# Two-layer mixture-of-experts trunk on one core: rows stored by index into expert slots while routing, plain loads and stores per expert, results fetched by token at the end

## The chip, the cores and the metric

The kernel runs on one core of a Trainium2 chip. The time is that of the device for one execution, in microseconds (us). Engines: PE multiplies matrices, DVE and ACT work on vectors, POOL (GpSimd) on vectors and on DMAs by index, SP only issues DMAs. The DMAs of all queues are carried out by the core's 16 DMA engines.

## The reference, cut to what matters

Two layers work on 512 latent tokens and 256 context tokens of width 1024. Each layer has a token mixer and then a mixture of 32 experts, of which each token takes two. In the last layer the experts see the latent tokens alone.

```python
def hier_moe(h, rg_w, rg_b, re_w, re_b, w_gate, w_up, w_down):
    g_top = jnp.argmax(g_logits, axis=-1)
    ...
    top_vals, top_idx = lax.top_k(e_in, TOP_K)
    top_w = jax.nn.softmax(top_vals, axis=-1) * g_w
    expert_idx = g_top[:, None].astype(jnp.int32) * EXPERTS_PER_GROUP + top_idx.astype(jnp.int32)
    ...
    def run_block(args):
        tok, e = args
        xb = h_pad[tok]
        return (jax.nn.silu(xb @ w_gate[e]) * (xb @ w_up[e])) @ w_down[e]
    ...
    return jax.ops.segment_sum(y_buf, buf_tok, num_segments=T + 1)[:T].astype(h.dtype)
...
        x = x + g2 * y[:B * T].reshape(B, T, D)
        ctx_h = ctx_h + cg2 * y[B * T:].reshape(B, n_ctx, D)
...
    return rms_norm(x, final_norm_g)
```

## The kernel before

The order of the work on each engine is written out by hand. All weights come through one list of 1 MB loads on SP's queue: `pump` issues the next of them into the pool R, seven buffers of 8 KB per partition, as far ahead as `st["depth"]` allows. Each expert has six such loads, 6.29 MB. A load becomes two half-precision parts: ACT writes the high part (L1335), DVE the low part (L1340), and each product of the gate and up matrices is three matmuls (`mm3`, L418 to L420). Half of the down matrix is used as it came (L1283).

A layer runs so. `out_and_route` makes the mixer's output projection tile by tile (128 tokens, six tiles in layer 0, four in layer 1), the residual, the second norm and the router. For each tile `choose` finds the two experts on DVE; `positions` counts with small matmuls which place a token has in its expert. The normalized rows, a high and a low half-precision part of 2 KB each, are stored in token order to the DRAM tensor `hs[l]` on SP's queue (L865), the residual stream to `xs[l]` on ACT's.

`moe` then runs 32 experts. An expert has 96 slots (`CAP`); experts with more tokens go through `overflow_blocks`, which this input doesn't need. Expert 0's rows are picked by matmuls. For the others, two tables turn the routing round: `slots` builds on DVE and PE the list of tokens for each slot, `values` the weight of each slot. POOL fetches an expert's rows by index (`fetch`, L1214; slots without a token move nothing), PE turns them (L1226), and gate, up and down follow, each expert's down product beside the next one's gate. `down_out` scales by the slot's weight on ACT, POOL builds the gate row for latent and context tokens (L1294, L1295, layer 0 alone), multiplies by it (L1303) and adds the rows to `xs[l]` by an indexed DMA that reads and writes (L1307). At the end the latent rows are loaded from `xs[l]`, and the last expert's rows are added by matmuls with a selection matrix (`add_last`, L1456, L1459). After layer 0 the rows are normalized and transposed for the next mixer (L488, L476, L464); after layer 1 they are normalized and written out (L1704).

The pools: G, 14 large buffers for converted weights, fetched rows (`xg`) and results (`ye`); R, seven raw loads; W, small tiles.

## Time and profile before

| | before |
|---|---|
| median of 3 runs | 1858.94 us (1855.53 to 1868.47) |
| the profiled execution | 1856.79 us |
| its span, first to last instruction | 1855.0 us |
| busy: PE, DVE, ACT, POOL | 1609.5, 1330.5, 1020.3, 1032.4 us |
| moved by DMA | 542.31 MB, mean 292 GB/s |

Busy times are of one engine each and lie beside each other; only the work that the end waits for sets the time. The gate activation of expert 0 (L1261) starts at 376.0 us in layer 0 and at 1248.4 in layer 1, that of expert 31 at 952.9 and 1814.8. The stretches in the rows below are cut at gate activations.

### The profile page before, as it was taken

How to read it: one execution, taken by the hardware profiler on the slowest of the kernel's cores; microseconds unless marked ns; L12 is line 12 of the kernel's file. 1: busy time of each engine (PE TensorE's matmuls, PEld its weight loads, DVE VectorE, ACT ScalarE, POOL GpSimd, SP SyncE). 2: the span in 40 equal slices, each digit the busy share in tenths (PEclk: the TensorE clock that was granted, in tenths of full speed). 3: DMA queues.
4: the chain of work that ended last, by engine and by line, in shares of the span. 5: the costliest groups of instructions: out<-in, count | busy, mean ns of one | idle time of the engine just before them, and what ended most of it. 6: DMA issues, size and time to landing. Idle time of an engine off the chain costs nothing. (4 is left out here: it accounts for less than half of the span.)

```text
span 1855.0 us, 43386 instructions
## 1 busy us (share of the span) xinstructions
PE 1609.5 (87%) x19059; PEld 1179.5 (64%) x19059; DVE 1330.5 (72%) x1451; ACT 1020.3 (55%) x1040; POOL 1032.4 (56%) x526
## 2 busy tenths in 40 slices
PE   6999999868888888888878999887888888889885
PEld 3567775556666666666654677566676666667663
DVE  5665567878789767777776877787767776666764
ACT  4433342446665666666654444346666666666662
POOL 1222234547898889998894333252554555454553
PEclk9999999889999999999998999988999999989998
DMA  9644564579998999999983455667999999999993
GB/s 386 234 159 155 183 227 153 174 231 375 382 359 326 383 364 344 370 358 361 364 318 143 136 196 180 269 213 268 377 366 348 378 354 369 352 357 357 360 348 116
DMA packets 123293, 542.31 MB, mean 292 GB/s; under 512 B 17594, under 2 KB 18666, under 8 KB 87000
## 3 DMA queue, kind: packets, MB, share of 16 engines
q1 hardware_dynamic: 105384, 507.87, 73.0%
q0 software_dynamic: 14000, 20.54, 4.7%
q10 hardware_dynamic: 3712, 11.04, 1.5%
q8 instruction: 153, 2.51, 0.5%
q14 instruction: 44, 0.36, 0.1%
...
## 5 line engine op out<-in xcount | busy, mean ns | idle before, releaser
L1340 DVE SCALAR_TENSOR_TENSOR wlo<-raw,whi 128x2048 f16<-128x2048 f32 x248 | 589.3, 2410 | 216.5 <-ACT whi L1335 216.4
L1335 ACT ACTIVATE whi<-raw 128x2048 f16<-128x2048 f32 x248 | 472.8, 1910 | 316.8 <-DMA raw<-in_exp_w_up_dram 279.3
L420 PEld LDWEIGHTS <-wlo 128*128 128x128 f16 x4512 | 458.3, 102 | 175.6 <-issue 144.5
L418 PEld LDWEIGHTS <-whi 128*128 128x128 f16 x4512 | 459.1, 102 | 45.9 <-issue 16.6
L419 PEld LDWEIGHTS <-whi 128*128 128x128 f16 x4512 | 458.8, 102 | 40.4 <-issue 11.2
L419 PE MATMUL pgate<-xl,whi 128*128 128x96 f16 x2048 | 308.1, 220 | 132.8 <-ACT xl L1234 132.5
L418 PE MATMUL pgate<-xh,whi 128*128 128x96 f16 x2048 | 312.1, 220 | 5.0 <-DVE xh L1233 4.8
L1303 POOL TENSOR_TENSOR ye<-ye,modrow 96x512 f32<-96x512 f32 x62 | 163.0, 2628 | 264.4 <-ACT ye L1287 264.4
L420 PE MATMUL pgate<-xh,wlo 128*128 128x96 f16 x2048 | 308.1, 220 | 0.0
L418 PE MATMUL pup<-xh,whi 128*128 128x96 f16 x2048 | 266.3, 206 | 0.0
L420 PE MATMUL pup<-xh,wlo 128*128 128x96 f16 x2048 | 266.1, 206 | 0.0
L419 PE MATMUL pup<-xl,whi 128*128 128x96 f16 x2048 | 266.0, 206 | 0.0
L1283 PE MATMUL pdn<-raw,sg 128*96 128x512 f32 x512 | 243.9, 599 | 0.0
L1307 POOL DMA_INDIRECT xs<-ye,si x63 | 171.4, 2721 | 21.5 <-POOL ye L1303 17.3
L1340 DVE SCALAR_TENSOR_TENSOR wd<-raw,wd 128x2048 f16<-128x2048 f32 x64 | 163.2, 2549 | 16.5 <-ACT wd L1335 16.3
L1294 POOL TENSOR_SCALAR ye<-modrow,sv 96x1024 f32<-96x1024 f32 x32 | 162.3, 5073 | 1.4
L1303 POOL TENSOR_TENSOR ye<-ye 96x512 f32<-96x512 f32 x62 | 134.7, 2183 | 49.3 <-ACT ye L1287 47.3
L1283 PEld LDWEIGHTS pdn<-raw,sg 128*96 128x96 f32 x512 | 85.2, 166 | 89.7 <-issue 71.1
L1335 ACT ACTIVATE wd<-raw 128x2048 f16<-128x2048 f32 x64 | 122.2, 1910 | 21.1 <-DMA raw<-in_exp_w_down_dram 21.1
L418 PE MATMUL pdn<-wd,at 128*96 128x512 f16 x256 | 100.1, 391 | 20.8 <-ACT at L1271 11.1
L1214 POOL DMA_INDIRECT xg<-hs,si x62 | 94.3, 1521 | 36.8 <-issue 23.2
L405 DVE SCALAR_TENSOR_TENSOR wlo<-raw,whi 128x2048 f16<-128x2048 f32 (+1 forms) x36 | 82.8, 2305 | 40.2 <-ACT whi L404 40.2
...
## 6 DMA issues: line engine op xcount, KB each, us to landing
raw<-in_exp_w_gate_dram SPq DMA_DIRECT2D x128, 1024.0 KB
raw<-in_exp_w_up_dram SPq DMA_DIRECT2D x128, 1024.0 KB
raw<-in_exp_w_down_dram SPq DMA_DIRECT2D x128, 1024.0 KB
...
```

Of the source, the lines that this page charges most:

```text
L405: V.scalar_tensor_tensor(lo, t, WS, hi, op0=ALU.mult, op1=ALU.subtract)
L418: T.matmul(o, lhsT=lh, rhs=rh, start=first, stop=False)
L419: T.matmul(o, lhsT=lh, rhs=rl, start=False, stop=False)
L420: T.matmul(o, lhsT=ll, rhs=rh, start=False, stop=last)
L1214: Q.indirect_dma_start(out=xg[0:CAP], out_offset=None, in_=hs[l], in_offset=bass.IndirectOffsetOnAxis(ap=si, axis=0), bounds_check=(6 - 2 ...
L1283: T.matmul(pt[0:CAP, :], lhsT=sg[:, f, :], rhs=raw[:, f - 2, sl], start=False, stop=(f == 3))
L1294: Q.tensor_scalar(gn, g2r[0:CAP, 1, :], ctx, None, op0=ALU.mult)
L1303: eng.tensor_tensor(yn, yn, gs[n], op=ALU.mult)
L1307: Q.indirect_dma_start(out=xs[l], out_offset=bass.IndirectOffsetOnAxis(ap=si, axis=0), in_=yg[0:CAP, 0, :], in_offset=None, bounds_check=6 ...
L1335: A.activation(hi[:, sl, :], t, AF.Copy, scale=WS)
L1340: V.scalar_tensor_tensor(lo, t, WS, hi, op0=ALU.mult, op1=ALU.subtract)
```

## The change

The DRAM tensor `hs` now has a row of 4 KB for each of 32 x 96 slots and serves both layers. `clear_rows` fills it with zeros in the first mixer, in eight DMAs on ACT's queue. `positions` runs tile by tile and gives each token its two slots (`si`; beyond the end for a token without a place), and `dispatch` stores the tile's rows there with two indexed DMAs from POOL; the store in token order remains, to `hn[l]`. `slots`, `values` and the tables are gone; the token's two weights are made at e = 4 (`weights`). `fetch` is a plain load of the expert's 96 rows, on SP's queue (the first two on POOL's). `down_out` scales by a constant, and `keep_rows` stores all 96 result rows plainly to `ys[l]` on ACT's queue. At the end `collect` fetches for each tile the two result rows of every token by index, and `combine` weights them, adds them, multiplies by the gate row and adds the residual: one pass on ACT and three on DVE per tile. The last expert's rows still come through matmuls in the latent tiles (`sel_last`); in layer 0 two context tiles are combined behind them. `finish` puts each tile's final norm between the combinations. The depth of the weight loads falls to 2 near the end of a layer, since the collected rows lie in pool R.

```diff
-    hs = [pd.tile([(6 - 2 * l) * 128, 2 * D], F16, name=f"hs{l}") for l in range(DEPTH)]
+    hs = pd.tile([NE * CAP, 2 * D], F16, name="hs")
+    hn = [pd.tile([(6 - 2 * l) * 128, 2 * D], F16, name=f"hn{l}") for l in range(DEPTH)]
+    ys = [pd.tile([NE * CAP, D], F32, name=f"ys{l}") for l in range(DEPTH)]
...
+    def clear_rows(q):
+
+        e0, r = 8 * (q // 2), q % 2
+        nc.scalar.dma_start(
+            out=hs.rearrange("(e p) (r d) -> p e r d", p=CAP, r=2)[:, e0:e0 + 8, r, :],
+            in_=zrow.unsqueeze(1).to_broadcast([CAP, 8, D]))
...
+            if l == 0 and 5 <= n < 13:
+                clear_rows(n - 5)
...
+        def dispatch(i):
+
+            for k in range(2):
+                Q.indirect_dma_start(
+                    out=hs, out_offset=bass.IndirectOffsetOnAxis(ap=rt.si[:, i, k:k + 1], axis=0),
+                    in_=h2[i // 2][:, i % 2].rearrange("p r d -> p (r d)"), in_offset=None,
+                    bounds_check=NE * CAP - 1, oob_is_err=False)
+            store_rows(i)
...
             if i > 1:
-                store_rows(i - 2)
+                rt.positions(i - 2)
+                dispatch(i - 2)
             resid(i, 1, V)
...
-        store_rows(i - 1)
         rt_mm(i, True)
-        rt.positions(0, i)
+        rt.positions(i - 1)
...
         low = norm2(i, True)
-        rt.positions(i, nt)
+        dispatch(i - 1)
+        rt.positions(i)
         make_sel(pe, rt.posm[:, :, 0:1], (i,), V)
         low()
-        store_rows(i)
+        dispatch(i)
...
+        def positions(self, i):
+
+            t, oh = self.tmp[:, i], self.oh
+            pos = P([128, 512], "pos")[:, 0:32]
+            for j in range(i + 1):
+                T.matmul(pos, lhsT=(tri16 if j == i else ones16), rhs=oh[:, j, :], start=(j == 0), stop=(j == i))
+            o = t[:, 120:184].rearrange("p (k e) -> p k e", k=2)
+            pk, sf, dead = self.pk[:, i], self.sf[:, i], t[:, 184:186]
+            V.tensor_tensor(o, o, pos.unsqueeze(1).to_broadcast([128, 2, 32]), op=ALU.mult)
+            V.tensor_reduce(pk, o, axis=AX.X, op=ALU.add)
+            V.tensor_scalar(dead, pk, CAP - 0.5, 65536.0, op0=ALU.is_gt, op1=ALU.mult)
+            V.scalar_tensor_tensor(sf, self.ef[:, i], float(CAP), pk, op0=ALU.mult, op1=ALU.add)
+            V.tensor_tensor(sf, sf, dead, op=ALU.add)
+            V.tensor_copy(self.si[:, i], sf)
+            V.scalar_tensor_tensor(self.posm[:, i], pos, 1.0, oh[:, i], op0=ALU.add, op1=ALU.mult)
...
+    def fetch(xg, e, eng=nc.sync):
+
+        eng.dma_start(out=xg[0:CAP], in_=hs[e * CAP:e * CAP + CAP, :])
...
-    def scatter_rows(l, yg, si):
-        Q.indirect_dma_start(
-            out=xs[l], out_offset=bass.IndirectOffsetOnAxis(ap=si, axis=0),
-            in_=yg[0:CAP, 0, :], in_offset=None, bounds_check=6 * 128 - 1, oob_is_err=False,
-            compute_op=ALU.add)
+    def down_out(pt, y, n):
+        A.activation(y[0:CAP, n * 512:(n + 1) * 512], pt[0:CAP, :], AF.Copy, scale=IWS)
+
+    def keep_rows(l, e, y):
+        nc.scalar.dma_start(out=ys[l][e * CAP:e * CAP + CAP, :], in_=y[0:CAP])
+
+    def collect(l, yt, rows, i, n):
+
+        for k in range(2):
+            Q.indirect_dma_start(
+                out=yt[:, k], out_offset=None, in_=ys[l][0:n * CAP],
+                in_offset=bass.IndirectOffsetOnAxis(ap=rows[:, i, k:k + 1], axis=0),
+                bounds_check=n * CAP - 1, oob_is_err=False)
+
+    def combine(xx, yt, w, i, g2row):
+
+        A.activation(yt[:, 0], yt[:, 0], AF.Copy, scale=w[:, i, 0:1])
+        V.scalar_tensor_tensor(yt[:, 0], yt[:, 1], w[:, i, 1:2], yt[:, 0], op0=ALU.mult, op1=ALU.add)
+        V.tensor_tensor(yt[:, 0], yt[:, 0], g2row, op=ALU.mult)
+        V.tensor_tensor(xx, xx, yt[:, 0], op=ALU.add)
...
-        rt.slots()
         for e in (1, 2):
-            fetch(l, xg[:, e % 2], slot(e))
+            fetch(xg[:, e % 2], e, Q)
...
-        rt.values()
         hi_(1, 1, 1)
...
+            yg = rows_of(e)
+            if e + 3 < NE:
+                fetch(xg[:, (e + 1) % 2], e + 3)
             if e == NE - 2:
-                st["depth"] = NR - 2
+                st["depth"] = 2
...
-            scatter(l, yg, slot(e), gs, Q)
+            down_out(pt, yg, 1)
+            keep_rows(l, e, yg)
...
         overflow_blocks()
+        yts = []
+        for i in range(4):
+            yts.append(R([128, 2, D], F32, "yt"))
+            collect(l, yts[i], rt.sa, i, NE - 1)
...
+        for i in range(4):
+            xx = xl[i // 2][:, i % 2]
+            combine(xx, yts[i], rt.wa, i, g2r[:, 0])
+            for n in range(2):
+                sl = slice(n * 512, (n + 1) * 512)
+                pt = P([128, 512], "pcm")
+                T.matmul(pt, lhsT=selT[0:CAP, i * 128:(i + 1) * 128], rhs=yh[n][0:CAP], start=True, stop=True)
+                V.tensor_tensor(xx[:, sl], pt, xx[:, sl], op=ALU.add)
+            finish(i, xx)
+        finish(4, None)
+        if nv == 2:
+            for i in (4, 5):
+                yt = R([128, 2, D], F32, "yt")
+                collect(l, yt, rt.sa, i, NE)
+                combine(xl[2][:, i % 2], yt, rt.wa, i, g2r[:, 1])
```

Where the change moves instructions, the order shows it at three places. POOL's row from the end of layer 0's routing into the expert loop, before (`h` are the normalized rows, `xg` the fetched ones, `ye` the results, `modrow` the gate rows):

```order
L861 TENSOR_TENSOR h_2_3367<-h2f,h_2_3367 128x512
L1486 MEMSET xg 96x2048
L1214 DMA xg<-hs_81,si_2720 96x2048 x2
L1498 TENSOR_TENSOR modrow<-modrow 128x1024
L1294 TENSOR_SCALAR ye<-modrow,sv_2721 96x1024
L1295 TENSOR_TENSOR ye<-ye,modrow 96x1024
L1303 TENSOR_TENSOR ye<-ye 96x512 x2
L1307 DMA xs_79<-ye,si_2720 768x1024
```

And with the change (`rsi` are the slots of the tokens; L403 and L1331 are the norm's power step and the load of the overflow count at the loop's end):

```order
L883 DMA hs<-h_1_3186,rsi_2735 3072x2048 x2
L403 TENSOR_TENSOR ss<-ss,mhalf 128x1
L863 TENSOR_TENSOR h2f<-h2f,modrow 128x512
L864 TENSOR_TENSOR h2f<-h2f,modrow 128x512
L873 TENSOR_TENSOR h_2_3435<-h2f,h_2_3435 128x512
L883 DMA hs<-h_2_3435,rsi_2735 3072x2048 x4
L1204 DMA xg<-hs 96x2048 x2
L1331 TENSOR_LOAD nov_2738
```

The two fetches now stand behind four indexed stores, the last of which needs the last tile's slots, and nothing of POOL is left in the loop.

POOL's row from the end of layer 0's loop (a branch) to the transposes of the next layer, before:

```order
L1355 UNCONDITIONAL_BRANCH
L1446 TENSOR_TENSOR yh<-ye,yh 96x512
L1307 DMA xs_79<-ye,si_2720 768x1024
L400 TENSOR_TENSOR ss<-ss,mhalf 128x1 x4
L448 TENSOR_TENSOR hTl<-hmod,hTh 128x512 x4
```

And with the change (`yt` are collected rows):

```order
L1337 UNCONDITIONAL_BRANCH
L1282 DMA yt<-ys_84,rsa_2736 128x1024 x8
L403 TENSOR_TENSOR ss<-ss,mhalf 128x1 x4
L1282 DMA yt<-ys_84,rsa_2736 128x1024 x4
L451 TENSOR_TENSOR hTl<-hmod,hTh 128x512 x4
```

Eight gathers for the latent tiles come first, and the four of the context tiles stand behind the four power steps of the latent tiles' norms.

DVE's row from the last down product of layer 1 to the end, before:

```order
L1444 SCALAR_TENSOR_TENSOR ye<-pdn,sv_15018,modrow 96x512 x2
L1446 TENSOR_TENSOR yh<-ye,yh 96x512
L1459 TENSOR_TENSOR xl<-pcm,xl 128x512 x8
L399 TENSOR_SCALAR ss<-ss 128x1 x2
L1704 SCALAR_TENSOR_TENSOR xl<-xl,ss,fg 128x1024
L399 TENSOR_SCALAR ss<-ss 128x1
L1704 SCALAR_TENSOR_TENSOR xl<-xl,ss,fg 128x1024
L399 TENSOR_SCALAR ss<-ss 128x1
L1704 SCALAR_TENSOR_TENSOR xl<-xl,ss,fg 128x1024 x2
```

And with the change, for the first two of four tiles:

```order
L1565 SCALAR_TENSOR_TENSOR yh<-pdn,modrow 96x512 x2
L1290 SCALAR_TENSOR_TENSOR yt<-yt,rwa_14842 128x1024
L1291 TENSOR_TENSOR yt<-yt,modrow 128x1024
L1292 TENSOR_TENSOR xl<-xl,yt 128x1024
L1578 TENSOR_TENSOR xl<-pcm,xl 128x512 x2
L402 TENSOR_SCALAR ss<-ss 128x1
L1290 SCALAR_TENSOR_TENSOR yt<-yt,rwa_14842 128x1024
L1291 TENSOR_TENSOR yt<-yt,modrow 128x1024
L1292 TENSOR_TENSOR xl<-xl,yt 128x1024
L1578 TENSOR_TENSOR xl<-pcm,xl 128x512 x2
L402 TENSOR_SCALAR ss<-ss 128x1
L1700 SCALAR_TENSOR_TENSOR xl<-xl,ss,fg 128x1024
```

All of `combine` stands behind the last down product's passes (`yh`), and each tile has three passes of 1024 columns more.

## Rows read from the trace of the kernel before

**Rows 1.** The page: busy time, 40 slices of PE and DMA.
```profile
PE 1609.5 (87%) x19059; PEld 1179.5 (64%) x19059; DVE 1330.5 (72%) x1451; ACT 1020.3 (55%) x1040; POOL 1032.4 (56%) x526
...
PE   6999999868888888888878999887888888889885
...
DMA  9644564579998999999983455667999999999993
```

**Rows 2.** 26 experts per layer: us, PE, PEld, DVE, ACT, POOL, clock, DMA, GB/s.
```profile
457.10:939.70 482.60, 412.11 (x5939) 321.79 (x5938) 375.55 (x254) 310.81 (x261) 438.85 (x159) 0.95 0.98 362
1321.20:1798.30 477.10, 412.13 (x5937) 323.26 (x5936) 331.31 (x252) 310.31 (x261) 249.69 (x107) 0.95 0.97 360
```

**Rows 3.** Waits in the stretch of layer 1: total us, times, longest.
```profile
ACT whi L1335 <- DMA raw<-in_exp_w_up_dram: 130.0, 37, 5.8
```

**Rows 4.** DMA queues, layer 0: packets, MB, share of 16 engines.
```profile
q1 hardware_dynamic: 29186, 164.02, 88.8%
q0 software_dynamic: 5824, 9.72, 8.3%
```

**Rows 5.** DMA queues in the stretch of layer 1.
```profile
q1 hardware_dynamic: 29211, 164.06, 90.7%
q0 software_dynamic: 5842, 6.72, 5.9%
```

**Rows 6.** PE where the loops start, timeline: start, us, [idle before].
```profile
393.40 0.71 PE L1116 MATMUL ptab<-rwt,ph 128*96 128x96 f16 x6 [12.57 <-DVE rwt L1145]
...
395.90 1.48 PE L1226 MATMUL pgx<-ident,xg 96*128 96x96 f16 x16
...
1261.21 1.48 PE L1226 MATMUL pgx<-ident,xg 96*128 96x96 f16 x16
```

**Rows 7.** GB/s in 40 slices of 376 to 424 us, 1.2 us each.
```profile
GB/s 393 432 440 434 420 335 321 311 253 270 317 294 96 0 0 0 0 0 7 0 14 198 396 280 116 300 423 75 143 277 314 277 202 249 263 406 335 406 365 427
```

**Rows 8.** DVE before the first expert of layer 0, timeline.
```profile
369.61 0.69 DVE L860 TENSOR_TENSOR h<-h2f,h 128x512 f16<-128x512 f32 x1
...
373.07 0.35 DVE L1097 TENSOR_REDUCE rtmp<-rtmp 128x6 f32<-128x192 f32 x1
```

**Rows 9.** POOL's groups in layer 0's stretch: busy us, mean ns, idle before.
```profile
L1307 POOL DMA_INDIRECT xs<-ye,si x25 | 75.7, 3026 | 7.0 <-POOL ye L1303 7.0
...
L1214 POOL DMA_INDIRECT xg<-hs,si x26 | 39.6, 1524 | 8.0 <-issue 7.0 <-PE pgate L420 0.9
```

**Rows 10.** SP and POOL at the start of layer 1, timeline.
```profile
1240.65 1.48 SPq L865 DMA_DIRECT2D hs<-h  x2
...
1250.43 2.16 POOL L1214 DMA_INDIRECT xg<-hs,si  x1 [9.06 <-DMA hs<-h]
```

**Rows 11.** Stretches of the mixer and of two routing tiles, layer 0.
```profile
150.00:250.00 100.00, 100.00 (x905) 72.57 (x903) 58.24 (x87) 37.13 (x59) 24.08 (x24) 1.00 0.40 146
313.00:328.70 15.70, 15.70 (x87) 8.62 (x86) 12.35 (x23) 3.48 (x6) 9.12 (x7) 1.00 0.17 67
328.70:344.20 15.50, 12.22 (x71) 7.20 (x69) 12.29 (x20) 5.17 (x7) 8.06 (x6) 1.00 0.38 128
```

**Rows 12.** DVE at the end of layer 0, timeline.
```profile
977.45 1.41 DVE L1444 SCALAR_TENSOR_TENSOR ye<-pdn,sv,ye 96x512 f32<-96x512 f32 x2 [5.17 <-POOL ye L1295]
...
988.38 0.75 DVE L488 TENSOR_SCALAR xl<-xl,ss 128x1024 f32<-128x1024 f32 x1 [0.63 <-POOL ss L400]
...
992.58 1.53 DVE L464 TENSOR_SCALAR hmod<-xT,abT 128x512 f32<-128x512 f32 x2 [0.60 <-PE xT L476]
```

**Rows 13.** DVE at the end of layer 1, timeline.
```profile
1836.62 0.75 DVE L1444 SCALAR_TENSOR_TENSOR ye<-pdn,sv,modrow 96x512 f32<-96x512 f32 x1 [2.27 <-PE pdn L1283]
...
1838.67 4.87 DVE L1459 TENSOR_TENSOR xl<-pcm,xl 128x512 f32<-128x512 f32 x8
...
1844.29 1.28 DVE L1704 SCALAR_TENSOR_TENSOR xl<-xl,ss,fg 128x1024 f32<-128x1024 f32 x1 [0.63 <-POOL ss L400]
...
1847.28 2.48 DVE L1704 SCALAR_TENSOR_TENSOR xl<-xl,ss,fg 128x1024 f32<-128x1024 f32 x2 [0.38 <-POOL ss L400]
```

More of the change, by code (lines that the diff above doesn't have):

```diff
@@ L1075, in choose @@
             V.scalar_tensor_tensor(self.oh[:, i], iot32, ef[:, 1:2], o1, op0=ALU.is_equal, op1=ALU.add)
-        def positions(self, i0, i1):
-            nt, oh = i1 - i0, self.oh
-            pos = P([128, 512], "pos")[:, 0:nt * 32].rearrange("p (t e) -> p t e", e=32)
-            for i in range(i0, i1):
-                for j in range(i + 1):
-                    T.matmul(pos[:, i - i0, :], lhsT=(tri16 if j == i else ones16), rhs=oh[:, j, :],
-                             start=(j == 0), stop=(j == i))
-            V.scalar_tensor_tensor(self.posm[:, i0:i1], pos, 1.0, oh[:, i0:i1], op0=ALU.add, op1=ALU.mult)
@@ L1111, in table @@
-        def table(self, rs, n):
-            nt = self.nt
-            pt = P([128, 512], "ptab")[0:CAP, 0:n]
-            for k in range(2):
-                for i in range(nt):
-                    T.matmul(pt, lhsT=self.ph[k][:, i, :], rhs=rs[k][:, i],
-                             start=(k == i == 0), stop=(k == 1 and i == nt - 1))
-            return pt
-        def values(self):
-            nt, tmp, oh, v4 = self.nt, self.tmp, self.oh, self.v4
-            g0, o1, o2, tv = tmp[:, :, 56:60], tmp[:, :, 120:152], tmp[:, :, 152:184], tmp[:, :, 184:216]
+            V.tensor_scalar(o2, iot32, ef[:, 1:2], None, op0=ALU.is_equal)
@@ new lines, in overflow_blocks @@
+                    m, t2 = (wt[:, 2 * nt * k:2 * nt * k + 2 * nt].rearrange("p (t k) -> p t k", k=2) for k in range(2))
+                    pb, vf = wt[:, 4 * nt:5 * nt], wt[:, 5 * nt:6 * nt]
+                    V.tensor_scalar(m, rt.ef, bc[:, 1:2], None, op0=ALU.is_equal)
+                    V.scalar_tensor_tensor(t2, rt.pk, 1.0, m, op0=ALU.add, op1=ALU.mult)
+                    V.tensor_tensor(pb, t2[:, :, 0], t2[:, :, 1], op=ALU.add)
+                    V.tensor_scalar(pb, pb, bc[:, 3:4], None, op0=ALU.subtract)
@@ L1382, in overflow_blocks @@
+                    for q in range(3):
+                        V.tensor_copy(vb[:, :, q + 1], vf)
+                        V.tensor_tensor(vf, vf, vb[:, :, q + 1], op=ALU.subtract)
                     pe = W([128, nt, CAP], F16, "pe")
-                    make_sel(pe, pb, range(nt))
-                    sv, si = slot_vals(pe, lambda i: vb[:, i, :], nt)
-                    fetch(l, xg[:, 0], si[0:CAP, :1])
+                    make_sel(pe, pb.unsqueeze(2), range(nt))
+                    sv, si = slot_vals(pe, vb, nt)
@@ L1449, in add_last @@
-        def add_last(selT, yh):
-            for i in range(4):
-                for n in range(2):
-                    sl = slice(n * 512, (n + 1) * 512)
-                    pt = P([128, 512], "pcm")
-                    for r in range(2):
-                        T.matmul(pt, lhsT=selT[0:CAP, i * 128:(i + 1) * 128], rhs=yh[0:CAP, r, sl],
-                                 start=(r == 0), stop=(r == 1))
-                    xx = xl[i // 2][:, i % 2, sl]
-                    V.tensor_tensor(xx, pt, xx, op=ALU.add)
@@ L1514, in moe @@
                 xe = turned(xt_)
-            down_out(pt, weight(0), yg[:, 0, :], n)
+            down_out(pt, yg, n)
+        keep_rows(l, 0, yg)
         lo_()
-        scatter(l, yg, slot(0), gs, Q)
         pgt = P([128, 4, CAP], "pgate")
@@ L1534, in moe @@
         hi_(2, 1, 1)
-        for e in (3, 4):
-            fetch(l, xg[:, e % 2], slot(e))
+        fetch(xg[:, 1], 3)
         xe = xn
-        pes = None
         for e in range(1, NE):
@@ L1566, in moe @@
             pt = down_mm(w, raw, at, sgd, 0)
-            down_out(pt, weight(e), yg[:, 0, :], 0)
+            down_out(pt, yg, 0)
             if nx2:
@@ L1587, in moe @@
             xe = xn
+            if e == 4:
+                rt.weights()
             if e == 8:
@@ L1673, with finish0 @@
     h2, rt, pe0 = out_and_route(0, mix, job, 6)
-    xt = moe(0, h2, rt, pe0, 6)
-    xt.append(G([128, 2, D], F32, "x"))
-    nc.sync.dma_start(out=xt[2], in_=xs[0][512:768, :].rearrange("(t p) d -> p t d", p=128))
-    norm_in_place(xt[:2])
+    xt = [G([128, 2, D], F32, "x") for _ in range(2)]
+    fin = []
+    def finish0(i, xx):
+        if i < 0:
+            return
+        if i < 4:
+            ss = rms(xx)
+            nc.scalar.dma_start(out=xs[0][i * 128:(i + 1) * 128, :], in_=xx)
+        if i:
+            V.tensor_scalar(xt[(i - 1) // 2][:, (i - 1) % 2], fin[0], fin[1], None, op0=ALU.mult)
+        if i < 4:
+            fin[:] = xx, ss
+    xt.append(moe(0, h2, rt, pe0, 6, finish0))
     hT = alloc_hT()
```

259 lines of the change are left out of this document (101 added, 158 removed).

## The prediction

> **What bounds the kernel now.** I read the page first: no engine is full over the span, PE is highest at 87%, but the slices show the DMA engines at nine tenths in two long runs with PE below nine [rows 1]. These are the expert loops. Stretches cut from one expert's gate activation to another's, 26 experts each, show the DMA engines busy for 98% and 97% of the time, PE for 412 of 482.6 and 412 of 477.1 us [rows 2]. So an expert takes 18.56 us in layer 0 and 18.35 in layer 1, while PE works 15.9 of it. The waits say the same from the engines' side: ACT's conversion of the weights waits for their DMA, 130 us in layer 1 alone [rows 3]. POOL, the engine that the change empties, is busy for 439 of 482.6 us in layer 0 but only 250 in layer 1 [rows 2], and the loop is as slow there: POOL doesn't set the pace, and its 17 us per expert buy nothing when they go. **The loops are bound by the DMA engines, so the change is priced in DMA time.**
>
> The queue views split that time. In layer 0, q1 (weights) has 88.8% of the engines for 164.02 MB, q0 (indexed fetch and adding scatter) 8.3% for 9.72 MB; in layer 1, q1 90.7%, q0 5.9% for 6.72 MB [rows 4, 5]. Per expert: q1 16.5 and 16.6 us for 6.31 MB, which is 383 and 379 GB/s; q0 1.54 us for 0.37 MB and 1.08 us for 0.26 MB. q0 is dear per byte (243 GB/s), but moves only rows that hold a token.
>
> **The change part by part**, against the profiled execution's own 1856.8 us (span 1855.0; the median of the runs is 2.1 us above).
>
> *Loop.* The indexed fetch and the adding scatter become a plain load and a plain store of all 96 slots of 4 KB: 2 x 0.393 MB per expert, full or empty. At q1's 383 GB/s that is 2.05 us, in place of 1.54 and 1.08: +0.51 us in layer 0 and +0.97 in layer 1. The engines are 97.5% busy, so nearly all of it lengthens the period: +0.52 and +1.0 us for some 29 experts in the bound part of each loop, 15 + 29, of which I take **+40**. From below: if the idle 2 to 3% (0.4 and 0.5 us) closed entirely, +0.1 and +0.5 us would be left, +16. From above, +75 (first rival). What leaves POOL (gate rows, products, descriptors) counts zero: nothing waits for it. keep_rows on ACT's queue and the fetch on SP's add an issue each, under a microsecond (1.48 for two in [rows 10]), on engines with slack. The fetch stands on SP's queue between weight loads; its buffer was read by PE's transposes before the previous up product, so it should not hold the weights behind it. The weights of the routing move to e = 4 with an activation-table load, under the weights' DMA.
>
> *Start of a loop.* Before, PE waits 12.57 us in layer 0 for DVE's value tables, then turns the fetched rows at 395.9 [rows 6], and the DMA engines stand still from about 391 to 400 us [rows 7]. Both tables go. But the fetch now waits for scatters that are issued last: DVE ends the last low half at 370.3 [rows 8]; two calls of `positions`, each seven instructions in a chain where one stood (0.35 us at most [rows 8], an estimated 0.27 each: 1.6 more), delay it by about 3.2 us; the two last scatters cost POOL some 1.5 us each (the indexed fetch averages 1.52 in the loop, the adding scatter 3.0 [rows 9]), so they are out at 376.5. Landing: in layer 1 the row stores issued at 1240.65 release POOL's fetch at 1250.43 [rows 9, 10], 8.3 us from the end of issue. Then the load itself, 1.5 us of issue and an estimated 5 to land beside the weights: 391.3, so the turn is 4 us earlier. In layer 1 the same distances from the row stores [rows 10] end at about 1263, where the turn stands at 1261.2 [rows 6]: nothing gained. Weight buffers come free earlier, since DVE no longer builds tables between conversions, so I take **-8** for both; -29 if all of the DMA engines' lost time came back (an estimated 18 us from the slices of [rows 7] below 380 GB/s, and 11 in layer 1), +8 if the landings take longer.
>
> [...]
>
> *Routing tiles.* Per tile DVE gets 1.6 us more (above), POOL two scatters, 3 us. A tile takes 15.5 us with DVE at 12.3 and PE at 12.2, or 15.7 with PE full [rows 11]. Where PE is full, it hides; where PE waits for DVE's residual, it doesn't. Six tiles (the last two of each layer are in the term above) at 60%: **+6**, from 2 to 15.
>
> *Clearing.* Eight DMAs of 1.57 MB in the first mixer, 12.6 MB, 33 us at 383 GB/s. There the DMA engines are 40% busy and PE is at 100% [rows 11]: **+2**, from 0 to 10, if weight loads come late.
>
> *End of layer 1.* Before, DVE goes from the last down product (1837.37) to the last product (1849.76) in 12.4 us [rows 13]. Now each of four tiles takes three 1024-wide passes (1.28 us each, as L1704; twice the 0.69 of a 512-wide one at most [rows 8, 13]), two additions from PSUM (4.87 / 8 = 0.61 each [rows 13]) and L1704: 3.84 + 1.22 + 1.28 = 6.34, with the norm's small step 6.5: 26 in all, and 1 us for the last power step. In DVE's order they stand behind the last down product, so nothing runs ahead: **+15**, 12 to 18.
>
> *End of layer 0.* The same with a 0.75 us normalization [rows 12]. The last down product's two passes, which POOL's gate rows held until 978.86 [rows 12], end about 978; 978 + 4 x 6.0 + 1 = 1003. Then the two context tiles: POOL issues their gathers behind the four power steps, so at 1003: 4 x 1.5 us, 1 or 2 to land (an estimate), and the last combination, 3.84: 1014. DVE's first modulation, L464, then starts at 1014 where it was 992.58 [rows 12]: **+21**, 10 to 26. PE runs without a gap after that point, so the shift stays.
>
> Sum: 40 - 8 + 6 + 2 + 15 + 21 = +76, **1933 us**.
>
> **Rivals.**
> *Bytes, not packet time.* Both loops move the same 362 and 360 GB/s [rows 2] with different shares of q0 [rows 4, 5]; if that is a ceiling on bytes, an expert of 6.31 + 0.79 + 0.03 = 7.13 MB takes 19.7 and 19.8 us, +1.15 and +1.45 for 29 experts each: +75 in place of +40, so 1968. Against it: slices of [rows 7] reach 420 to 440 GB/s. [...]
> *The loop hardly grows.* The idle 2 to 3% takes the extra, and the drained time at the starts comes back: +16 - 29 + 6 + 2 + 15 + 21 = +31: 1888.
> *Faster.* The adding scatter, which reads and writes, slows the packets of the weights too; without it the engines run at the 427 GB/s of a good slice [rows 7] and an expert takes 7.13 MB / 427 = 16.7 us: -1.8 us for 58 experts, -104, and +36 from the rest: 1789. It decides from a period of 17.8 us (58 x 0.62 = 36). Against it: layer 1 has a third less q0 traffic, and its weights took 16.6 us per expert, not less than 16.5 [rows 4, 5].
> *It doesn't come down as said:* a fetch on SP's queue waits (for its buffer, or the scatters) and holds the weight loads behind it; 1 us for each of 58 experts would give 1991.
>
> **How the numbers follow.** Forecast 63%, bytes 13%, hardly grows 12%, faster 6%, the held queue 3%, the remainder within 1% of before by several savings at once, 3%. The range 1882 to 1972 holds the forecast's bounds, 1888 and 1968. Faster by over 1% (what a measurement here tells from no change) 0.06, within 1% 0.06, slower 0.88.
>
> **What would show it.** The queue view of the loops: q0 gone, q1 and q10 with 7.1 MB per expert, DMA still at 97% and a period of 19.1 to 19.4 us in both layers alike; 18.5 or less would make the loop's term wrong. PE's turn at the start of layer 0 not before 388 us plus what routing adds. DVE at the ends with rows of 1.28 us one after the other, and nothing of them ahead of the last down product. If POOL's scatters or the clearing turn up as waits of PE, those terms were too small.

## The result and the profile after

| | before | changed |
|---|---|---|
| median of the runs | 1857.24 us (1852.61 to 1868.47, 4 runs) | 2032.2 us (2028.63 to 2037.68, 4 runs) |
| span of the profiled execution | 1855.0 us | 2030.7 us |

The ratio is 1.0935, with a 95% interval of 1.0879 to 1.099: slower, and by more than twice what was forecast. On the page of the changed kernel POOL is nearly empty, as foreseen (1032.4 us before, [rows 1]), and PE's share falls from 87 to 81%, since it waits more; the slices of the DMA engines are still at nine tenths in both expert loops.

```profile
PE 1648.7 (81%) x19019; PEld 1213.8 (60%) x19019; DVE 1304.1 (64%) x1497; ACT 1024.0 (50%) x1048; POOL 257.6 (13%) x244
...
DMA  9588464679999999999962455668999999999983
```

Windows of 26 experts, cut at the gate activations of experts 4 and 30 as in [rows 2] (columns: length, busy time of PE, PEld, DVE, ACT and POOL, granted clock, DMA share, GB/s):

```profile
477.97:992.85 514.88, 423.67 (x5943) 334.28 (x5942) 334.71 (x269) 310.77 (x266) 0.00 (x0) 0.93 1.02 363
1436.70:1956.80 520.10, 427.50 (x5948) 336.97 (x5947) 334.95 (x266) 312.02 (x266) 0.00 (x0) 0.92 1.02 358
```

The period is 514.88 / 26 = 19.80 us in layer 0 and 20.00 in layer 1 (18.56 and 18.35 before). The DMA engines are full, POOL does nothing, and the rate is again 363 and 358 GB/s, as in [rows 2]. The queue view of layer 0's window (packets, MB, share of 16 engines), beside [rows 4]:

```profile
q1 hardware_dynamic: 32349, 175.75, 95.9%
q10 hardware_dynamic: 2912, 10.23, 5.2%
```

The store's queue q10 takes 5.2% of 514.88 / 26 us, 1.03 us per expert, as priced. But q1, weights and fetch, takes 19.0 us for 6.76 MB: 356 GB/s, where q1 with the weights alone had 383 before. Within one period the rate is not even. GB/s in 40 slices of 1 us, from 614 to 654 us:

```profile
GB/s 397 410 442 422 410 410 451 406 287 205 274 369 254 229 258 328 397 430 430 397 422 406 414 434 434 418 406 369 295 258 320 303 324 254 250 410 401 414 418 422
```

It runs at 400 to 450, and once in each period, for some eight slices, at 205 to 370. SP issues a fetch at 614.81 and the next at 634.51, each behind weight loads issued before it; the slow slices begin 7 us later. The trace shows the slowing in the weights' own packets, which are the 8 KB ones: over layer 0's window they take 317 to 328 ns on average in the first 4 us after a fetch is issued, 403 to 437 between 6 and 16 us after it, and 318 to 332 from then to the next fetch.

The start of layer 0's loop on POOL (start, duration, instruction, idle time before and its releaser), and PE's turn of expert 1's rows, which [rows 6] has at 395.9:

```profile
385.74 1.30 POOL L883 DMA_INDIRECT hs<-h,rsi  x1 [0.17 <-issue]
396.37 0.97 POOL L883 DMA_INDIRECT hs<-h,rsi  x1 [9.33 <-DMA hs<-h,rsi]
404.97 0.97 POOL L883 DMA_INDIRECT hs<-h,rsi  x1 [7.62 <-DMA hs<-h,rsi]
408.56 0.97 POOL L883 DMA_INDIRECT hs<-h,rsi  x1 [2.62 <-DMA hs<-h,rsi]
412.46 1.12 POOL L1204 DMA_DIRECT2D xg<-hs  x2 [2.94 <-DMA hs<-h,rsi]
```

```profile
416.24 1.46 PE L1213 MATMUL pgx<-ident,xg 96*128 96x96 f16 x16 [18.83 <-DMA xg<-hs]
```

Each indexed store waits until the one before it has landed: 9.33, 7.62 and 2.62 us, and then the fetch waits 2.94 for the last. The line's own view says the same for the whole program (12 waits of the store for a store, 68.1 us):

```profile
L883 POOL DMA_INDIRECT hs<-h,rsi x20: 961/982/1304, 317.3 to 1367.3; - x20
...
  DMA hs<-h,rsi: 68.1, 12
```

In the routing, POOL's power step of the norm stands behind such a store, and DVE waits for it, as in this tile of layer 0:

```profile
322.95 3.11 DVE L866 SCALAR_TENSOR_TENSOR h2f<-xr,ss,modrow 128x512 f32<-128x512 f32 x2 [2.60 <-POOL ss L403]
```

The end of layer 0 on DVE, beside [rows 12]: the last pass of the down product ends at 1034.46, the first combination starts 5.37 us later, a tile takes 1047.27 - 1039.82 = 7.45 us, the context tiles wait 6.82 us for their rows, and the first modulation starts at 1084.92. POOL issues the first of the eight gathers only at 1031.67, just behind the down product's first pass.

```profile
1033.77 0.69 DVE L1565 SCALAR_TENSOR_TENSOR yh<-pdn,modrow 96x512 f32<-96x512 f32 x1 [2.33 <-PE pdn L1270]
1039.82 1.28 DVE L1290 SCALAR_TENSOR_TENSOR yt<-yt,rwa 128x1024 f32<-128x1024 f32 x1 [5.37 <-DMA yt<-ys,rsa]
1041.14 1.22 DVE L1291 TENSOR_TENSOR yt<-yt,modrow 128x1024 f32<-128x1024 f32 x1
1042.40 1.23 DVE L1292 TENSOR_TENSOR xl<-xl,yt 128x1024 f32<-128x1024 f32 x1
1043.73 1.29 DVE L1578 TENSOR_TENSOR xl<-pcm,xl 128x512 f32<-128x512 f32 x2
1046.23 0.15 DVE L402 TENSOR_SCALAR ss<-ss 128x1 f32<-128x1 f32 x1 [1.21 <-ACT sqj L401]
1047.27 1.28 DVE L1290 SCALAR_TENSOR_TENSOR yt<-yt,rwa 128x1024 f32<-128x1024 f32 x1 [0.89 <-ACT yt L1289]
...
1077.48 1.28 DVE L1290 SCALAR_TENSOR_TENSOR yt<-yt,rwa 128x1024 f32<-128x1024 f32 x1 [6.82 <-DMA yt<-ys,rsa]
...
1084.92 2.24 DVE L467 TENSOR_SCALAR hmod<-xT,abT 128x512 f32<-128x512 f32 x3
```

The end of layer 1 on DVE, beside [rows 13]: 32.3 us from the last pass of the down product to the last product, where 12.4 stood.

```profile
1993.63 0.69 DVE L1565 SCALAR_TENSOR_TENSOR yh<-pdn,modrow 96x512 f32<-96x512 f32 x1 [2.27 <-PE pdn L1270]
1994.23 1.27 DVE L1290 SCALAR_TENSOR_TENSOR yt<-yt,rwa 128x1024 f32<-128x1024 f32 x1
...
2001.72 1.29 DVE L1290 SCALAR_TENSOR_TENSOR yt<-yt,rwa 128x1024 f32<-128x1024 f32 x1 [0.89 <-ACT yt L1289]
...
2025.34 1.28 DVE L1700 SCALAR_TENSOR_TENSOR xl<-xl,ss,fg 128x1024 f32<-128x1024 f32 x1 [0.44 <-POOL ss L403]
```

By stretches between the same marks in both traces:

| stretch | forecast | measured |
|---|---|---|
| experts 4 to 30, both layers (482.6 to 514.9, 477.1 to 520.1 us) | +36 | +75.2 |
| up to expert 4's gate activation: mixers, routing, starts of the loops (+20.9 and +23.1) | 0 | +44.0 |
| end of layer 0, from expert 31's gate activation to the first modulation (39.7 to 76.9) | +21 | +37.2 |
| end of layer 1, from there to the end (40.2 to 59.0) | +15 | +18.8 |
| experts 30 to 31 | +4 | +0.5 |
| sum | +76 | +175.7 |

The forecast of the loop, +40, is shared out here over 29 experts. Within the second row, +17.4 and +12.6 us lie ahead of expert 0's gate activation, +3.5 and +10.5 behind it. The loops alone came out as the rival "bytes, not packet time" had it (19.7 and 19.8 us), and my first theory was that one: a ceiling on bytes. The rivals to it: the fetch is dear in itself, by its place in SP's queue, by its memory reads, or by where its rows go.

### The profile page after: what moved, and what is told of

Its sections match the earlier page's. It is cut to its first block, busy times and chain, and to the rows that moved or that the text cites. A ratio compares the mean times of both kernels' runs of the same rounds, so it can differ in the third digit from the quotient of the medians.

```text
span 2030.7 us, 42983 instructions
## 1 busy us (share of the span) xinstructions
PE 1648.7 (81%) x19019; PEld 1213.8 (60%) x19019; DVE 1304.1 (64%) x1497; ACT 1024.0 (50%) x1048; POOL 257.6 (13%) x244
## 5 line engine op out<-in xcount | busy, mean ns | idle before, releaser
L1322 DVE SCALAR_TENSOR_TENSOR wlo<-raw,whi 128x2048 f16<-128x2048 f32 x248 | 565.7, 2289 | 317.1 <-ACT whi L1317 316.7
L422 PEld LDWEIGHTS <-whi 128*128 128x128 f16 x4512 | 470.3, 104 | 61.5 <-issue 32.7
L421 PEld LDWEIGHTS <-whi 128*128 128x128 f16 x4512 | 470.8, 104 | 46.1 <-issue 17.4
L422 PE MATMUL pgate<-xl,whi 128*128 128x96 f16 x2048 | 332.6, 228 | 181.3 <-ACT xl L1221 181.0
L421 PE MATMUL pgate<-xh,whi 128*128 128x96 f16 x2048 | 336.6, 228 | 10.1 <-DVE xh L1220 10.0
L423 PE MATMUL pgate<-xh,wlo 128*128 128x96 f16 x2048 | 332.7, 228 | 0.0
L1282 POOL DMA_INDIRECT yt<-ys,rsa x20 | 20.7, 1037 | 1233.4 <-DVE yh L1565 618.1
L421 PE MATMUL pjl<-hTh,whi 128*128 128x512 f16 x256 | 98.8, 386 | 16.5 <-ACT hTh L468 11.5
L421 PE MATMUL pdn<-wd,at 128*96 128x512 f16 x256 | 99.1, 387 | 12.1 <-PEq L1337 9.7
L422 PE MATMUL pjl<-hTl,whi 128*128 128x512 f16 x256 | 98.5, 385 | 3.6 <-DVE hTl L451 3.6
L1213 PEld LDWEIGHTS <-xg 96*128 96x128 f16 x992 | 50.3, 100 | 81.2 <-DMA xg<-hs 47.7
L422 PE MATMUL pdn<-wd,at 128*96 128x512 f16 x256 | 98.7, 386 | 0.0
```

The costliest lines, as they stand in the source:

```text
L421: T.matmul(o, lhsT=lh, rhs=rh, start=first, stop=False)
L422: T.matmul(o, lhsT=lh, rhs=rl, start=False, stop=False)
L423: T.matmul(o, lhsT=ll, rhs=rh, start=False, stop=last)
L1213: T.transpose(pt[:, c, :], xg[0:CAP, o:o + 128], ident16[0:CAP, 0:CAP])
L1282: Q.indirect_dma_start(out=yt[:, k], out_offset=None, in_=ys[l][0:n * CAP], in_offset=bass.IndirectOffsetOnAxis(ap=rows[:, i, k:k + 1], ax ...
L1322: V.scalar_tensor_tensor(lo, t, WS, hi, op0=ALU.mult, op1=ALU.subtract)
```

## The experiments

Periods are those of experts 4 to 30, in layer 0 and layer 1.

**Without the store.**

```diff
-            V.tensor_tensor(self.sa, self.sf, keep, op=ALU.mult)
+            V.tensor_scalar(self.sa, self.sf, 0.0, None, op0=ALU.mult)
...
-            keep_rows(l, e, yg)
```

> The changed kernel without the plain store of each expert's 96 result rows for experts 1 to 30 (the rows collected at the end all come from expert 0, so the output is left out in part). An expert moves 6.79 MB in place of 7.18. If the loop is held by a ceiling on bytes of some 360 GB/s: period 18.7 us in layer 0 and 18.95 in layer 1 (19.80 and 20.00 with the store). If the store costs only its packets' own time (1.03 us of the 16 engines): 18.8 and 19.0, which is no different; if stores to memory are dear beside loads: below 18.3; if the fetch on SP's queue holds the weights back: 19.5 or more. Time near 1965 us.

Measured: 1980.17 us, periods 18.85 and 18.91. Layer 0's window:

```profile
479.30:969.38 490.08, 417.09 (x5938) 327.76 (x5937) 334.73 (x270) 308.99 (x266) 0.00 (x0) 0.94 1.01 360
```

The store costs 0.95 and 1.09 us, about its packets' own time. The rate stays at 360 and 358 GB/s, so a ceiling on bytes was still possible.

**Without store and fetch.** As above, and:

```diff
-        fetch(xg[:, 1], 3)
...
-            if e + 3 < NE:
-                fetch(xg[:, (e + 1) % 2], e + 3)
```

> The changed kernel without the plain store and without the plain fetch from expert 3 on (experts compute on old rows, the end collects rows of expert 0). An expert moves 6.40 MB. Ceiling on bytes of 358 to 363 GB/s: period 17.6 us in layer 0 and 17.9 in layer 1. Packet time alone (weights as before the change, 16.5 and 16.6 us of the 16 engines): 16.5 to 16.9. PE's own work would allow 16.0 to 16.4.

Measured: 1785.34 us, periods 15.38 and 15.39. Both windows:

```profile
474.88:874.81 399.93, 390.79 (x5936) 303.05 (x5935) 330.10 (x270) 305.20 (x266) 0.00 (x0) 1.00 1.02 413
1308.16:1708.34 400.18, 390.69 (x5934) 302.96 (x5933) 329.65 (x267) 305.58 (x265) 0.00 (x0) 1.00 1.02 413
```

The same weights now come at 413 GB/s, and PE is busy for 98% of the time, at a granted clock of 1.00 where it had 0.93. The DMA engines are full as well, so this run doesn't tell which of the two holds it; the weights need no more than its period. **The ceiling on bytes is refuted**, and so is the base of the forecast: 16.5 us was not what the weights need. Their queue in layer 0's window:

```profile
q1 hardware_dynamic: 29223, 164.21, 100.7%
```

That is 15.5 us of the 16 engines per expert, where q1 took 19.0 with the fetch. The fetch costs at least 18.85 - 15.38 = 3.47 us in layer 0 and 3.52 in layer 1, for the same 0.39 MB that cost 1 us as a store.

**Fetch from the chip's own memory.**

```diff
-        fetch(xg[:, 1], 3)
+        nc.sync.dma_start(out=xg[0:CAP, 1], in_=xg[0:CAP, 0])
...
-                fetch(xg[:, (e + 1) % 2], e + 3)
+                nc.sync.dma_start(out=xg[0:CAP, (e + 1) % 2], in_=xg[0:CAP, e % 2])
```

> The changed kernel with the fetch of 96 rows from expert 3 on replaced by a copy of the same 96 x 4 KB from the other fetch buffer on the chip (the rows are the wrong ones): the same packets for the DMA engines, but no reading from memory. If the ceiling is on what is read from and written to memory: period 18.7 us in layer 0 and 18.95 in layer 1. If the DMA engines' own time or the queue's order is the limit: 19.8 and 20.0 as with the fetch.

Measured: 2040.07 us, periods 19.83 and 19.95; layer 0's window:

```profile
481.54:997.25 515.71, 423.12 (x5943) 333.79 (x5942) 334.00 (x269) 311.35 (x265) 0.00 (x0) 0.93 1.01 362
```

The loop is as slow as with the fetch (19.80 and 20.00), so it is not the reading of `hs`. Both kernels share how the fetch writes: 96 partitions, on SP's queue.

**Fetch of 128 rows.** More bytes, in the weights' shape:

```diff
-        eng.dma_start(out=xg[0:CAP], in_=hs[e * CAP:e * CAP + CAP, :])
+        n = CAP if e == NE - 1 else 128
+        eng.dma_start(out=xg[0:n], in_=hs[e * CAP:e * CAP + n, :])
```

> The changed kernel with each fetch (but the last) widened from 96 to 128 rows, into 128 partitions, as the weight loads go; the 32 rows more are the next expert's and are not used. It moves 0.13 MB more per expert. If the fetch is dear (3.5 us per expert, from the two runs without it) because its 96 partitions fall on other DMA engines than the weights' 128, and the engines then meet at the same partitions: the period falls from 19.8 and 20.0 to some 17.4 us (7.2 MB at the 413 GB/s of the run with weights alone), the weights' 8 KB packets take near 318 ns on average again (365 now), time near 1885 us. If the fetch is dear for its bytes or its place in the queue: 20.1 us and more, 2040 us.

Measured: 1911.15 us (1908.94 to 1915.16), ratio to before 1.0314 (1.0271 to 1.0358), periods 17.64 and 17.64. Both windows, and the same 40 slices as above:

```profile
475.60:934.13 458.53, 406.97 (x5947) 317.17 (x5946) 333.24 (x269) 308.32 (x265) 0.00 (x0) 0.97 1.02 412
1372.85:1831.61 458.76, 405.78 (x5939) 317.31 (x5938) 332.64 (x266) 308.59 (x265) 0.00 (x0) 0.97 1.02 413
```

```profile
GB/s 438 393 414 414 426 442 410 406 422 422 426 406 406 410 414 414 410 422 414 430 406 434 422 410 434 414 414 397 406 430 406 414 422 406 418 406 438 410 406 442
```

A third more rows, and the loop gains 2.2 and 2.4 us per expert: the slow slices are gone, and 412 GB/s is kept throughout. The weights' 8 KB packets now take 313 to 322 ns at any distance from a fetch. Relative to the run without fetch and store, the period grows by 2.26 us for 0.92 MB, 406 GB/s: now the transfers cost what their bytes cost at the rate of the weights. Both loops are also shorter than in the kernel before (458.5 and 458.8 us for 26 experts against 482.6 and 477.1, 42.5 us in all); the starts and the ends, 93 us longer, keep this kernel slower.

**Fetch on ACT's queue.**

```diff
-    def fetch(xg, e, eng=nc.sync):
+    def fetch(xg, e, eng=nc.scalar):
```

> The changed kernel with the fetches issued on ACT's queue in place of SP's (and of POOL's for the first two). If the fetch is dear because it stands between the weight loads on their queue: period near 17.4 us. If it is dear by where its 96 rows go: 19.5 to 20 us, as now.

Measured: 1943.43 us, periods 18.27 and 18.30, between the two expectations. Layer 0's window:

```profile
477.75:952.68 474.93, 410.69 (x5931) 323.12 (x5930) 331.79 (x270) 308.57 (x266) 0.00 (x0) 0.95 1.02 392
```

On ACT's queue, which it shares with the stores, the narrow fetch costs some 1.6 us less, but the rate still stays at 392 GB/s. ACT also issues it at another moment, 2 us behind a store (617.91 after 615.79). So the place in the weights' queue, or the moment that goes with it, is a part of the cost; which of them, and by what mechanism, stays open.

**Fetch of 64 rows, and of 128 rows of 2 KB.** Equal bytes, 0.26 MB:

```diff
-        eng.dma_start(out=xg[0:CAP], in_=hs[e * CAP:e * CAP + CAP, :])
+        n = CAP if e < 3 else 64
+        eng.dma_start(out=xg[0:n], in_=hs[e * CAP:e * CAP + n, :])
```

> The changed kernel with 64 rows in place of 96 in each fetch from expert 3 on (rows 64 to 95 of an expert are old ones). By bytes or packets alone a third of the 3.5 us goes: period near 18.6 us. If the spread over partitions decides, 64 partitions are no better matched with the engines of the weights than 96: more than two thirds of the cost stays, 18.9 to 19.8 us.

```diff
-        eng.dma_start(out=xg[0:CAP], in_=hs[e * CAP:e * CAP + CAP, :])
+        if e < 3 or e == NE - 1:
+            eng.dma_start(out=xg[0:CAP], in_=hs[e * CAP:e * CAP + CAP, :])
+        else:
+            eng.dma_start(out=xg[:, 0:D], in_=hs[e * CAP:e * CAP + 128, 0:D])
```

> The changed kernel with each fetch from expert 3 to 30 as 128 rows of 2 KB (the high parts of the next rows; the low parts are old ones) in place of 96 rows of 4 KB: 0.26 MB, as many bytes as the run with 64 rows of 4 KB, which took 19.2 us per expert. If it is the number of partitions that decides: 6.29 + 0.26 + 0.39 MB and the small loads at the 415 GB/s of the run with 128 rows, 17.0 us per expert. If any narrow fetch of these bytes is as dear: 19 us.

Measured: 1998.39 us and periods 19.22 and 19.21 with 64 partitions; 1879.04 us and 17.08 and 17.11 with 128. Layer 0's windows, of the 64 rows and of the 128 thin ones:

```profile
478.23:977.99 499.76, 420.94 (x5936) 332.66 (x5934) 334.23 (x269) 310.69 (x266) 0.00 (x0) 0.92 1.01 366
```

```profile
475.44:919.42 443.98, 399.77 (x5965) 309.97 (x5964) 333.44 (x269) 307.95 (x265) 0.00 (x0) 0.99 1.02 412
```

Equal bytes, the same queue, the same place: 2.1 us per expert lie between 64 and 128 partitions. The rows differ too, 4 KB and 2 KB, but the 128 rows above had 4 KB and were cheap as well (17.64 us).

**Four row tensors.** No indexed store waits for another one of the last two tiles (the clearing becomes 32 transfers in place of 8):

```diff
-    hs = pd.tile([NE * CAP, 2 * D], F16, name="hs")
+    hs = [pd.tile([NE * CAP, 2 * D], F16, name=f"hs{t}") for t in range(4)]
...
-                    out=hs, out_offset=bass.IndirectOffsetOnAxis(ap=rt.si[:, i, k:k + 1], axis=0),
+                    out=hs[2 * (i % 2) + k], out_offset=bass.IndirectOffsetOnAxis(ap=rt.si[:, i, k:k + 1], axis=0),
...
-        eng.dma_start(out=xg[0:CAP], in_=hs[e * CAP:e * CAP + CAP, :])
+        eng.dma_start(out=xg[0:CAP], in_=hs[(4 - e) % 4][e * CAP:e * CAP + CAP, :])
```

> The changed kernel with four row tensors in place of one: each of a tile's two indexed stores, of even and odd tiles, goes to a tensor of its own, so no store waits for the one before it, and an expert's rows are fetched from one of the four (three quarters of the rows it should have are zero). If the waits of POOL for the landing of its own stores are what lengthens the routing: expert 0's gate activation in layer 0 at about 381 us (393.4 now, 376.0 before the change), the routing of layer 1 8 us shorter, expert 1's turn at about 400 us (416.2 now), time near 2000 us. If the added DVE work or the clearing does it: gains under 8 us, 2024 or more.

Measured: 2007.74 us. Expert 0's gate activation at 387.6 (393.4), expert 1's turn at 402.4 (416.2); in the marks of the table above 5.7 + 6.5 us less in layer 0's start and 5.0 + 6.3 in layer 1's (ahead of expert 0's gate activation, and behind it), 23.5 us in all. The first residual of layer 0 came 2.7 us later here (289.7 against 286.9), which hides as much of the gain. POOL at the start of layer 0:

```profile
377.76 1.07 POOL L884 DMA_INDIRECT hs<-h,rsi  x1 [0.17 <-DVE ref L1099]
379.13 1.05 POOL L884 DMA_INDIRECT hs<-h,rsi  x1 [0.30 <-issue]
382.88 2.29 POOL L884 DMA_INDIRECT hs<-h,rsi  x1 [2.70 <-issue]
385.48 0.97 POOL L884 DMA_INDIRECT hs<-h,rsi  x1 [0.30 <-issue]
397.54 1.11 POOL L1205 DMA_DIRECT2D xg<-hs  x2 [11.10 <-DMA hs<-h,rsi]
```

The stores follow each other at once; what remains is the landing of the last ones, for which the fetch waits 11.10 us. The waits of stores for stores are some 23.5 of the 44 us, or 26 without the later first residual; the expectation of over 30 was too high.

**The weighting ahead of the last down product in layer 1.**

```diff
+        if nv == 1:
+            for i in range(4):
+                combine(xl[i // 2][:, i % 2], yts[i], rt.wa, i, g2r[:, 0])
         yh = W([128, 512], F32, "yh"), W([128, 512], F32, "yh")
...
-            combine(xx, yts[i], rt.wa, i, g2r[:, 0])
+            if nv == 2:
+                combine(xx, yts[i], rt.wa, i, g2r[:, 0])
```

> The changed kernel with the weighting and adding of the collected rows in layer 1 (three passes of DVE for each of four tiles) put ahead of the last down product's passes on DVE, which waits there. From expert 31's gate activation to the end: 59.0 us now; about 51 if the serial passes of DVE behind the last down product are the price (some 8 us of them fit into its wait); 58 or more if the collected rows arrive too late.

Measured: 2040.23 us; from expert 31's gate activation to the end 56.0 us (59.0), a miss. DVE:

```profile
1999.75 1.28 DVE L1290 SCALAR_TENSOR_TENSOR yt<-yt,rwa 128x1024 f32<-128x1024 f32 x1 [5.43 <-DMA yt<-ys,rsa]
...
2014.61 1.28 DVE L1568 SCALAR_TENSOR_TENSOR yh<-pdn,modrow 96x512 f32<-96x512 f32 x2
2017.52 0.69 DVE L1582 TENSOR_TENSOR xl<-pcm,xl 128x512 f32<-128x512 f32 x1 [1.63 <-PE pcm L1581]
```

The collected rows arrive late (5.43 us of waiting), so the first pass starts at 1999.75, and the down product's passes, whose second half PE ended by 2004.2, come behind all twelve at 2014.61. The passes are serial on DVE in either order; this order saved 3 of the 8 us that were hoped for.

**All repairs together.** The 128-row fetch, the order of the last experiment, and:

```diff
-            for k in range(2):
-                Q.indirect_dma_start(
-                    out=hs, out_offset=bass.IndirectOffsetOnAxis(ap=rt.si[:, i, k:k + 1], axis=0),
...
             resid(i, 0, V if lastt else Q)
+            if pend:
+                scat(*pend.pop())
...
             square(i)
+            if i > 1:
+                scat(i - 2, 0)
+                store_rows(i - 2)
+                pend.append((i - 2, 1))
...
             keep_rows(l, NE - 1, yg)
+            for i in (4, 5):
+                ytc.append(G([128, 2, D], F32, "yt"))
+                collect(l, ytc[-1], rt.sa, i, NE)
```

> The changed kernel with the 128-row fetch, with the two indexed stores of a routing tile put at different places of POOL's row (so that the wait for the first one's landing falls on other work), with the rows collected for the context tiles before the latent tiles are finished, and with the weighting of layer 1 ahead of the last down product's passes. Of 1911 us with the 128-row fetch alone: 10 to 25 less by the stores, 5 to 8 by the context rows, 3 by the order at the end: about 1882. If POOL's waits only move: 1900 or more. In no case below before, since four serial combinations of 7.5 us stay at the end of both layers.

Measured: 1906.26 us (1901.74 to 1908.55), ratio to before 1.0265 (1.0231 to 1.0299): 5 us below the 128-row fetch alone, where some 30 were expected; the intervals of the two ratios overlap. POOL before layer 0's loop:

```profile
394.24 1.27 POOL L883 DMA_INDIRECT hs<-h,rsi  x1 [0.15 <-issue]
404.28 0.96 POOL L883 DMA_INDIRECT hs<-h,rsi  x1 [8.76 <-DMA hs<-h,rsi]
410.00 0.96 POOL L883 DMA_INDIRECT hs<-h,rsi  x1 [4.76 <-DMA hs<-h,rsi]
414.54 1.16 POOL L1217 DMA_DIRECT2D xg<-hs  x2 [3.59 <-DMA hs<-h,rsi]
```

The last four stores and the fetch are still a chain of landings; the fetch starts at 414.54, 2 us later than in the changed kernel, though the first residual of layer 0 was 4 us later too (291.0 against 286.9). So spreading the stores over the tiles gained nothing by the traces: up to expert 4's gate activation both layers together take 6.9 us more than with the 128-row fetch alone, and the chain at the end stays. The other two repairs came near what was expected: the end of layer 0 took 69.0 us in place of 74.6, the end of layer 1 56.5 in place of 60.0.

**The kernel before with 128 partitions.**

```diff
+            V.memset(self.si[CAP:128], 8192)
...
-            out=xg[0:CAP], out_offset=None, in_=hs[l],
+            out=xg, out_offset=None, in_=hs[l],
...
-                    fetch(l, xg[:, e % 2], slot(e + 4))
+                    fetch(l, xg[:, e % 2], rt.si[:, e + 4:e + 5])
```

> The kernel before the change with each indexed fetch given 128 indices and partitions in place of 96 (the 32 more are out of bounds and move nothing). If the spread of 96 rows over the DMA engines disturbs the weights here too: the period falls from 18.56 and 18.35 us by 0.5 to 2 us, the weights' 8 KB packets from 345 and 351 ns towards 318, time 1750 to 1830 us. If an indexed fetch is spread otherwise, or the adding stores are what disturbs: no change, within 1% of before.

Measured: 1847.63 us (1841.6 to 1850.17), ratio 0.993 (0.9898 to 0.9961): a little faster than before, and the fastest of the kernels that do all the work. Both windows, periods 18.22 and 18.02 in place of 18.56 and 18.35:

```profile
463.94:937.74 473.80, 414.95 (x5936) 324.71 (x5935) 379.75 (x254) 311.53 (x261) 439.78 (x155) 0.94 0.98 367
1322.20:1790.80 468.60, 408.27 (x5937) 320.00 (x5936) 331.45 (x252) 309.98 (x261) 263.95 (x108) 0.96 0.98 367
```

The gain is 0.33 us per expert, below the 0.5 to 2 of the first case: the spread of the indexed fetch, as far as 128 indices change it, was not what holds the old loop.

**The kernel before without the adding stores.**

```diff
-            scatter(l, yg, slot(e), gs, Q)
+            for n in range(2):
+                yn = yg[0:CAP, 0, n * 512:(n + 1) * 512]
+                Q.tensor_tensor(yn, yn, gs[n], op=ALU.mult)
```

> The kernel before the change without the adding stores of experts 1 to 30 (their rows are left out of the sum); the products ahead of them stay. If the loop is held by the time of the packets of the DMA engines alone, the adding store's own share goes: from 18.56 and 18.35 us to some 17.5 in both layers. If the adding stores hold up the weights: 16.5 or less. If POOL's fetches alone disturb: 18 or more.

Measured: 1776.24 us, periods 17.71 and 16.41. Both windows:

```profile
455.48:916.06 460.58, 407.09 (x5936) 313.46 (x5935) 454.45 (x254) 303.98 (x261) 357.18 (x132) 0.97 0.98 367
1293.83:1720.40 426.57, 394.16 (x5933) 306.25 (x5932) 330.93 (x252) 306.93 (x262) 180.13 (x81) 0.99 1.01 394
```

In layer 1 the adding store costs 1.94 us per expert, and without it the loop runs at 394 GB/s. POOL's queue in layer 1's window, beside [rows 5]:

```profile
q0 software_dynamic: 2912, 3.39, 2.6%
```

Its share falls from 5.9% of 18.35 us to 2.6% of 16.41, which is 0.66 us per expert; the other 1.3 us are not the adding store's own packets. In layer 0 only 0.85 us come back: there DVE is next, with 454.45 of 460.58 us. Its 254 instructions took 375.55 us before; why they are longer here is not shown.

## Why the prediction was wrong

The direction was right, the size was not: +76 forecast, +175 measured, 2032 outside a range that ended at 1972. Of the 99 us between the two, 44 lie in the starts of the loops, 39 in the loops and 20 in the ends, less 4 between experts 30 and 31.

1. **The loop: the price of the fetch.** The step that failed is "at q1's 383 GB/s that is 2.05 us" for fetch and store. For the store it held (1.03 forecast, 0.95 and 1.09 measured). The fetch cost 3.5 us in place of 1.03, because each narrow load slows the weights' own packets: from 6 to 16 us after its issue the 8 KB ones take over 400 ns in place of some 320. The runs show that neither its bytes (128 rows: 17.64 us), nor its memory reads (copy on the chip: 19.83), nor its place in SP's queue alone (128 rows at the same place) makes that price, but the number of partitions it is spread over beside weights that go to 128 (64 rows of 4 KB 19.22, 128 of 2 KB 17.08); issued on ACT's queue, the narrow fetch still cost more than its bytes (18.27). By what mechanism the number of partitions sets the price stays open: no trace here shows which DMA engine moves a packet, or into which partitions, so that engines meet at the same partitions, as the expectation of the 128-row fetch has it, is not shown. For the queues the prediction counted no more than an issue each, under a microsecond. For this fetch that is not borne out: on ACT's queue, though at another moment as well, the period fell by 1.6 us, where the issue on SP's took 0.38.

2. **"The loops are bound by the DMA engines, so the change is priced in DMA time."** Full engines were read as the weights' need. With nothing beside them the weights take no more than 15.4 us, not 16.5: a busy share of 98% holds packets that are slowed by others. The share was 0.97 to 1.02 in all the loop windows above, at rates from 358 to 413 GB/s, so it doesn't tell what a loop needs. The rival "faster" had this mechanism, that the adding store slows the weights, and layer 1 of the kernel without it agrees (-1.94 us per expert, of which the store's own packets are 0.66). What it didn't have was that the new fetch costs more still (3.5 us per expert).

3. **"Bytes, not packet time"** came near the loop's figure (19.7 and 19.8 forecast, 19.80 and 20.00 measured) for a reason that the runs refute: the same engines move 413 GB/s. The equal rates of 360 GB/s were luck: in layer 1 the rate rose to 394 without the adding store in the kernel before, and to 413 with the wide fetch in the changed one.

4. **The start of the loops: -8 + 6 + 2 forecast, +44 measured.** "The two last scatters cost POOL some 1.5 us each" left out that a store into the tensor waits for the one before it (12 waits, 68.1 us). I counted their landing once, ahead of the fetch; it comes four times at the end and once in each earlier tile, on POOL, ahead of the norm's power step, for which DVE then waits (2.60 us in the tile shown). Separate tensors gave back some 23.5 us: 12.8 of the 14.0 behind expert 0's gate activation, but only 10.7 of the 30.0 ahead of it, where the forecast had +8 and the last two tiles' scatters and `positions`. The 5 us for the first fetch to land were an estimate that no row of before shows; in the changed kernel's trace the four fetches on POOL's queue landed 3.7 to 4.5 us after their issue. The first residual of layer 0 comes 2.4 us later (286.9 against 284.5 us), which agrees with the clearing's +2. The other 17 us or so ahead of expert 0 were not taken apart; the longer chain on DVE is a candidate that no run tests (the seven instructions of `positions` take 1.2 to 2.6 us in each of layer 0's tiles).

5. **The ends: +21 and +15 forecast, +37.2 and +18.8 measured.** The mechanism was right, three passes per tile behind the last down product; the tile was mis-sized, 7.45 us in layer 0 and 7.5 to 7.8 in layer 1 in place of 6.0 and 6.5, because ACT's square (1.06 us, then 0.19 to read it out) and DVE's wait for it (1.21 us) stand between the additions and the next tile's passes. In layer 0 two things come on top: a wait of 5.37 us for the first collected rows, which the forecast didn't have, and 3.7 us because both context tiles are combined behind the last wait, where it counted one. That last wait, 6.82 us for the context rows, is about what it had allowed in all (6 us to issue, 1 or 2 to land); the 1 or 2 us were an estimate that no run shows, and in the changed kernel's trace the gathers landed 4.4 to 7.4 us after their issue, 7.0 in the median of 20.

The step on POOL held: 775 us of its work went, and no stretch of the table got shorter. The chances don't add up as they stand: the four cases that end over 1% slower have 0.91 together, not 0.88, and the one within 1% has 0.03.
